# Second half of the Fourier gate computed between the second and the third branch, the Fourier branch stored ungated during the first block

## The chip, the cores and the metric

The kernel runs on one core of a Trainium2 chip. The core has five engines that work side by side, each through its own list of instructions in order: TensorE (PE, matmuls), VectorE (DVE), ScalarE (ACT), GpSimd (POOL) and SyncE (SP, which here only issues DMAs). The metric is the device time of one execution in microseconds (us).

## The reference

Two layers of a diffusion trunk over 512 sample tokens and 128 prompt tokens (640 columns), model width 1024, all in float32. In each layer the normalised hidden state `h` is projected by one wide matrix; three branches (retention, latent attention, Fourier mixing) are gated, projected and merged:

```
rq, rk, rv, rz, q_lat, kv_lat, k_r, mz, fu, fz, gl = jnp.split(h @ w_in, split_at, axis=-1)
o_r = retention(rq, rk, rv);  o_m = mla(q_lat, kv_lat, k_r);  o_f = fourier_mix(fu)
branches = jnp.stack([o_r * silu(rz), o_m * silu(mz), o_f * silu(fz)], axis=2)      # 3 x 512 wide
proj     = jnp.einsum('btnw,nwd->btnd', branches, w_branch)                         # 3 x 1024 wide
merged   = jnp.sum(proj * sigmoid(gl.reshape(B, T, 3, 1024)), axis=2)
x        = x + gate * (merged @ w_out)
```

## The kernel before

Everything lies transposed: features on the 128 partitions, tokens along the free axis. Each float32 operand is split into a rounded high part and a low rest (`split`: ACT casts the high part, `low` subtracts it on DVE or POOL, line 74), and each product is three matmuls (high x high, low x high, high x low).

A layer runs attention, retention, Fourier mixing, then the merge of the three branches, then the output projection. This case is about the passage from the Fourier mixing into the merge.

**The products of the merge.** `seven` makes 256 output features for all 640 tokens by seven block products in place of eight (a 2x2 block scheme: the weights and the tokens are added up beforehand). A block product of the hidden state is 12 matmuls of 128x320, so a gate (`gl`, or a quarter of `fz`) is 84 matmuls; a block product of a branch is 6, so a branch block is 42. `gl_weights` makes the weight sums of a gate from two loads (`raw`, `raw2`), `br_weights` those of a branch. The last two products of each `seven` are kept back in `tail` and run when `flush` is called, after the first product of the next one. `hq` holds the token sums of the hidden state. `branch_sums` makes the seven token blocks of a branch in place from its tile (lines 1008 to 1013) and splits each into two tiles: `bq0` to `bq9`, and four that don't fit and lie in `bql`. `bql` has the tag "of", the slot of the Fourier branch's own tile `oft`, so nothing can be written to `bql` before `oft` has been copied out to DRAM (`ofd`).

**The loops.** The Fourier branch has four groups of 128 features. `fourier` itself gates groups 0 and 1 (two `silu2`, line 954). Then one `seven` with its result in `zs` computes the gate of groups 2 and 3, `fourier_done` applies it (line 1234 and `fourier_gate`, line 954), and each group is stored to `ofd` (line 1236; groups 0 and 1 at line 1216). Then the merge: three branches in the order attention (n = 0, tile `omt`), retention (n = 1, tile `ort`) and Fourier (n = 2, loaded back from `ofd` into `ort` at line 1297), and for each of them four blocks of 256 output features: a gate (`seven`) and a branch product (`seven`, or `four` with 48 plain matmuls for n = 1). A gate's result is turned by ACT's tanh and multiplied in by DVE.

**What sets the order.** The source order is only a start: a list scheduler orders each engine's instructions when the program is built. Buffers rotate: `raw` 2, `raw2` 2, `wh` and `wl` (split weights) 4 each, `bank` (accumulators) 6, `th` 2. All loads of weights and all copies to and from `ofd` stand in SP's queue in order; the loads `mraw` of the modulation weights, which fill spare time on PE (line 187), stand in ACT's.

Of the kernel before, what the change touches and what calls it, by code (L numbers as in the profile page):

```python
# [8 lines left out]
F32 = mybir.dt.float32  # L9
# [21 lines left out]
def build(nc, tc, A, O):  # L31
# [806 lines left out]
    def fourier(l, fp, of, sums, wgp):  # L838
# [102 lines left out]
        ws = gl_weights(wgp, l, C_FZ + 256, lambda: z1.append(silu2(l, C_FZ + P, wz)))  # L941
# [50 lines left out]
    def branch_sums(gp, src, spare):  # L992
# [4 lines left out]
        t = t[:8] + x[:2] + t[8:] + x[2:]  # L997
# [195 lines left out]
    for l in range(DEPTH):  # L1193
# [21 lines left out]
        for w in range(2):  # L1215
            nc.sync.dma_start(ofd[:, w, :], oft[:, w, :])
# [3 lines left out]
        with ExitStack() as s:  # L1220
# [8 lines left out]
            zs = [fl.tile([P, TT], F32, name="tg", tag="th", bufs=2) for _ in range(2)]  # L1229

            def fourier_done(j):
                z, m, o = zs[j], mg[j], off[j + 2]
                ACT.activation(m, z, AF.Tanh, scale=0.5)
                DVE.scalar_tensor_tensor(m, m, 1.0, z, op0=ALU.add, op1=ALU.mult)
                fourier_gate(off, j + 2, m)
                nc.sync.dma_start(ofd[:, j + 2, :], o)

            seven(w0, hq, *zs, lambda ps: ACT.copy(zs[0][:, b], ps), fourier_done, lambda i: None)
# [6 lines left out]
            def gates(y2, n, bq, parts, np_):  # L1245
                def last(ps):
                    ACT.activation(y2[0][:, b], ps, AF.Tanh, scale=0.5)

                def fin(j):
                    y = y2[j][:, a] if j == 0 else y2[j]  # L1250
                    ACT.activation(y, y, AF.Tanh, scale=0.5)

                def tick(i):
                    if i in (3, 6):
                        next(steps, None)
                    if i % 2 and len(bq) < np_:
                        with tc.issue_after(gated.ins):
                            bq.append(next(parts))

                return last, fin, tick  # L1260
# [17 lines left out]
            for n, (idx, src, tmp) in enumerate(((1, omt, None), (0, ort, om), (2, ort, om))):  # L1278
                if n:
                    flush()  # L1280
                parts = branch_split(gp, src) if n == 1 else branch_sums(gp, src, bql)
                np_ = 4 if n == 1 else 7
                bq = []
                for i in range(4):
                    if n and i % 2 == 0:
                        y2 = tmp[2:4]
                    else:
                        y2 = [fl.tile([P, TT], F32, name="tg", tag="th", bufs=2) for _ in range(2)]
                    seven(gl_weights(wgp, l, C_GL + D * idx + 256 * i), hq, *y2, *gates(y2, n, bq, parts, np_))
# [176 lines left out]
```

## Time and profile before

| | us |
|---|---|
| median of 3 runs | 1479.51 (1477.54 to 1480.52) |
| the profiled execution's own time | 1482.52 |
| its span, first to last instruction | 1480.7 |

The profile is of one execution, 1.8 us outside its span and 3.0 us above the median. PE is busy for 96% of the span, DVE for 69%, ACT for 51%. The merge of layer 0 stands at about 431 to 710 us of the span, that of layer 1 at about 1153 to 1416 us. A row of the timeline begins with its start and its length, and a bracket at its end gives the idle time of the engine before it and what ended it.

### The profile page before, as it was taken

Reading aid. Unit: us, or ns where it says so; the run is one execution under the profiler, and the core shown is the slowest. Engines: PE = TensorE matmul, PEld = TensorE weight load, DVE = VectorE, ACT = ScalarE, POOL = GpSimd, SP = SyncE. Lnnn points to the kernel's source line nnn. Section 1 sums busy time; section 2 is a strip of 40 time slices with the busy share of each in tenths; the row PEclk is TensorE's granted clock in tenths of the full one; section 3 lists DMA queues with packets and bytes.
Section 4 is the critical chain, followed back from the end, with each engine's and each line's share of the span. In section 5 each row is a group of like instructions: output and inputs, shape, how many; then the busy total and the mean of one; then the engine's idle time right before and its main releaser. Section 6 shows DMA issues by size and latency. Waiting matters only on the chain.

```text
span 1480.7 us, 25121 instructions
## 1 busy us (share of the span) xinstructions
PE 1416.7 (96%) x9761; PEld 1346.9 (91%) x9761; DVE 1024.6 (69%) x1894; ACT 758.5 (51%) x1635; POOL 241.8 (16%) x227
## 2 busy tenths in 40 slices
PE   5999999999999999999999999999999999999997
PEld 3989989988897898999999899899889889999997
DVE  5367776667886686698573777765759768779843
ACT  6357666544544453455344566664545445445542
POOL 1220100301102111122312100021110112112240
PEclk9999999999999999999999999999999999999999
DMA  9520002421326464133532100042222424333342
GB/s 330 164 76 1 15 15 78 121 76 41 93 90 189 143 192 122 51 86 93 171 104 83 34 15 15 15 137 75 74 72 65 154 82 116 95 82 86 90 125 86
DMA packets 173735, 138.91 MB, mean 94 GB/s; under 512 B 8240, under 2 KB 164528, under 8 KB 173616
## 3 DMA queue, kind: packets, MB, share of 16 engines
q1 hardware_dynamic: 155568, 120.16, 28.0%
q10 hardware_dynamic: 18048, 17.15, 3.7%
q8 instruction: 77, 1.26, 0.4%
q14 instruction: 42, 0.34, 0.1%
HBM read 125.98 MB, written 11.30 MB: 93 GB/s over the span
## 4 chain that ended last, share of the span: by engine, by line
PE 72%; DVE 13%; DMA 6%; ACT 4%; issue 4%; POOL 1%; SPq 0%; POOLq 0%; DVEq 0%; ACTq 0%
PE bank L1109 25%; PE sm L85 5%; PE sm L87 5%; PE sm L86 5%; PE bank L1080 4%; PE big L513 4%; PE fill L319 3%; PE big L269 3%; PE sm L319 3%; PE sm L534 3%; DVE wl L74 2%; PE sm L526 2%; DMA mraw<-in_w_mod 2%; PE fill L187 1%; DMA raw<-in_w_in 1%
## 5 line engine op out<-in xcount | busy, mean ns | idle before, releaser
L74 DVE TENSOR_TENSOR wl<-raw,wh 128x1024 fp32r<-128x1024 f32 (+5 forms) x146 | 156.2, 1072 | 92.1 <-ACT wh L78 45.1
L78 ACT CAST wh<-raw 128x1024 fp32r<-128x1024 f32 (+5 forms) x126 | 104.4, 832 | 79.0 <-DMA raw<-in_w_in 18.1
L85 PE MATMUL sm<-wh,hh 128*128 128x256 f32 (+2 forms) x456 | 134.7, 296 | 0.4 <-DVE vl L74 0.4
L87 PE MATMUL sm<-wh,hl 128*128 128x256 f32 (+2 forms) x456 | 133.9, 294 | 0.9 <-DVE hl L74 0.9
L1109 PE MATMUL bank<-hh,wh 128*128 128x320 f32 x416 | 130.7, 316 | 4.0 <-ACT tg L1125 2.9
L86 PE MATMUL sm<-wl,hh 128*128 128x256 f32 (+2 forms) x456 | 134.5, 295 | 0.0
L1109 PE MATMUL bank<-hl,wh 128*128 128x320 f32 x416 | 129.5, 312 | 0.0
L1109 PE MATMUL bank<-hh,wl 128*128 128x320 f32 x416 | 127.8, 313 | 0.0
L74 POOL TENSOR_TENSOR wl<-raw,wh 128x1024 fp32r<-128x1024 f32 (+1 forms) x32 | 67.6, 2112 | 296.9 <-ACT wh L78 221.2
L74 POOL TENSOR_TENSOR wl<-st,wh 128x512 fp32r<-128x512 f32 x26 | 39.2, 1508 | 324.2 <-ACT wh L78 302.1
L85 PEld LDWEIGHTS sm<-wh,hh 128*128 128x128 f32 x456 | 88.2, 194 | 1.5 <-DVE vl L74 0.8
L87 PEld LDWEIGHTS sm<-wh,hl 128*128 128x128 f32 x456 | 88.0, 193 | 1.4 <-DVE hl L74 1.4
L86 PEld LDWEIGHTS sm<-wl,hh 128*128 128x128 f32 x456 | 88.4, 194 | 0.1
L1109 PEld LDWEIGHTS bank<-hh,wh 128*128 128x128 f32 x416 | 79.1, 190 | 9.9 <-ACT tg L1125 3.6
L1109 PEld LDWEIGHTS bank<-hl,wh 128*128 128x128 f32 x416 | 79.2, 190 | 0.0
L1109 PEld LDWEIGHTS bank<-hh,wl 128*128 128x128 f32 x416 | 78.7, 191 | 0.4 <-DVE raw L1025 0.4
L74 DVE TENSOR_TENSOR ptl<-sm,pth 128x384 fp32r<-128x384 f32 x128 | 67.4, 549 | 14.4 <-ACT pth L78 13.3
L1109 PE MATMUL bank<-bq,wh 128*128 128x320 f32 x320 | 72.1, 311 | 0.0
L78 ACT CAST pth<-sm 128x384 fp32r<-128x384 f32 x128 | 57.5, 480 | 24.1 <-PE sm L526 23.3
L78 ACT CAST wh<-st 128x512 fp32r<-128x512 f32 x68 | 39.7, 618 | 53.0 <-PE bank L1109 53.0
L640 DVE TENSOR_REDUCE nm<-big 128x1 f32<-128x768 f32 x64 | 60.7, 948 | 2.7 <-PE big L513 2.4
L74 DVE TENSOR_TENSOR wl<-st,wh 128x512 fp32r<-128x512 f32 x42 | 41.2, 980 | 30.2 <-ACT wh L78 27.7
(579 smaller groups left out, 4546.3 us busy)
## 6 DMA issues: line engine op xcount, KB each, us to landing
raw<-in_w_in SPq DMA_DIRECT2D x96, 512.0 KB, 4.0
mraw<-in_w_mod ACTq DMA_DIRECT2D x32, 512.0 KB, 4.3
raw<-in_w_branch SPq DMA_DIRECT2D x24, 512.0 KB, 3.6
raw<-in_w_out SPq DMA_DIRECT2D x16, 512.0 KB, 4.5
mraw<-in_w_mod SPq DMA_DIRECT2D x4, 1024.0 KB, 11.7
mraw<-in_w_mod SPq DMA_DIRECT2D x8, 512.0 KB, 8.3
raw<-in_w_in SPq DMA_DIRECT2D x8, 384.0 KB, 5.9
om<-xd SPq DMA_DIRECT2D x16, 192.0 KB, 3.1
```

The source lines that it names most:

```text
L74: eng.tensor_tensor(lo, src, hi.bitcast(F32), op=ALU.subtract)
L78: ACT.copy(hi, src)
L85: PE.matmul(out, ah, bh, start=first, stop=False)
L86: PE.matmul(out, ah, bl, start=False, stop=False)
L87: return PE.matmul(out, al, bh, start=False, stop=last)
L269: PE.matmul(ps[:, 512 * h:512 * h + 320], ws[a][:, k, :], xs[b][k][:, 320 * h:320 * h + 320], start=(first and k == 0 and i == 0), stop=(l ...
L319: PE.matmul(ps, w[a][:, k, :], (hh, hl)[b][k][:, hs], start=(k == 0 and i == 0), stop=(k == NK - 1 and i == 2))
L513: PE.matmul(S[:, 512 * h:512 * h + 384], qT[hd][a][:, t * P:(t + 1) * P], (kth, ktl)[b][hd % 3][:, 384 * h:384 * h + 384], start=(i == 0), ...
L534: PE.matmul(po[:, :256], vt[hd // 4][kt][:, hd % 4, :], pts[hd, qb][b][kt // 3][:, kt % 3, :], start=(kt == 0 and b == 0), stop=(kt == 5 a ...
L640: DVE.tensor_reduce(nm, Sv, axis=AX.XY if len(Sv.shape) == 3 else AX.X, op=ALU.max, negate=True)
L1080: PE.matmul(A, ws[u][:, k, j * P:(j + 1) * P], xs[k][v][:, h, :], start=(k == 0 and i == 0), stop=(k == 3 and i == 2))
L1109: PE.matmul(ps, w[u], x[v], start=(first and k == 0 and j == 0), stop=(k == n - 1 and j == 2), skip_group_check=True)
```

## The change

The gate of groups 2 and 3 is no longer computed ahead of the merge. `fourier` now loads the weights of the first gate of the merge in the place of those of the Fourier gate. The Fourier tile is stored to `ofd` with groups 2 and 3 ungated (group 0 and 1 are gated as before), by four DMAs that are issued in the first gate of n = 0, in the order 2, 3, 0, 1. The `seven` of the Fourier gate stands between n = 1 and n = 2, writes its result to `om[2]` and `om[3]` (free by then) and gates groups 2 and 3 in `ort`, after they were loaded back. Two smaller edits go with it: block 3 of `branch_sums` and not block 4 lies in `bql`, and in n = 0 every step of a gate may issue a part of `branch_sums`, not every second one. In n = 2 the gates of blocks 1 and 3, not 0 and 2, use `om[2:4]`.

```
@@ fourier
-        ws = gl_weights(wgp, l, C_FZ + 256, lambda: z1.append(silu2(l, C_FZ + P, wz)))
+        ws = gl_weights(wgp, l, C_GL + D, lambda: z1.append(silu2(l, C_FZ + P, wz)))
@@ branch_sums
-        t = t[:8] + x[:2] + t[8:] + x[2:]
+        t = t[:6] + x[:2] + t[6:] + x[2:]
@@ build
-        for w in range(2):
-            nc.sync.dma_start(ofd[:, w, :], oft[:, w, :])
...
-            zs = [fl.tile([P, TT], F32, name="tg", tag="th", bufs=2) for _ in range(2)]
...
-                z, m, o = zs[j], mg[j], off[j + 2]
+                z, m, o = om[2 + j], om[j], ort[:, 2 + j, :]
                 ACT.activation(m, z, AF.Tanh, scale=0.5)
                 DVE.scalar_tensor_tensor(m, m, 1.0, z, op0=ALU.add, op1=ALU.mult)
-                fourier_gate(off, j + 2, m)
-                nc.sync.dma_start(ofd[:, j + 2, :], o)
-
-            seven(w0, hq, *zs, lambda ps: ACT.copy(zs[0][:, b], ps), fourier_done, lambda i: None)
+                DVE.scalar_tensor_tensor(o, o, 0.5, m, op0=ALU.mult, op1=ALU.mult)
+
...
-                    if i % 2 and len(bq) < np_:
+                    if not n and not bq and not i:
+                        for w in (2, 3, 0, 1):
+                            nc.sync.dma_start(ofd[:, w, :], oft[:, w, :])
+                    if (i % 2 or not n) and len(bq) < np_:
...
+                if n == 2:
+                    seven(gl_weights(wgp, l, C_FZ + 256), hq, om[2], om[3], lambda ps: ACT.copy(om[2][:, b], ps), fourier_done, lambda i: None)
...
-                    if n and i % 2 == 0:
+                    if n and i % 2 == n - 1:
...
-                    seven(gl_weights(wgp, l, C_GL + D * idx + 256 * i), hq, *y2, *gates(y2, n, bq, parts, np_))
+                    seven(w0 if not (n or i) else gl_weights(wgp, l, C_GL + D * idx + 256 * i), hq, *y2, *gates(y2, n, bq, parts, np_))
```

In layer 0, SP's queue around the copies to `ofd` reads so before, with `in_w_branch` the weights of a branch block and `in_w_in` those of a gate:

```order
L92 DMA raw_5405<-in_w_branch 128x4x256
L1216 DMA ofd0_5103<-of_2986 128x640 x2
L92 DMA raw_5471<-in_w_in 128x8x128
L92 DMA raw_5601<-in_w_branch 128x4x256
L1236 DMA ofd0_5103<-of_2986 128x640
L1030 DMA raw2_5708<-in_w_in 128x8x128
L1236 DMA ofd0_5103<-of_2986 128x640
```

and now:

```order
L92 DMA raw_5275<-in_w_branch 128x4x256
L841 DMA traw_4568<-in_k_dftf 128x256
L1030 DMA raw2_5578<-in_w_in 128x8x128
L92 DMA raw_5341<-in_w_in 128x8x128
L1253 DMA ofd0_5103<-of_2986 128x640 x4
L92 DMA raw_5471<-in_w_branch 128x4x256
```

The four copies now stand together, ahead of the second branch block's weights.

In layer 1, ACT's list reads so at the start of the merge before (`wh_13338` are weights of the first gate, `bq6` and `bq2` high parts of the attention branch, L1117 and L1125 copies of a gate's product out of its accumulator):

```order
L1117 COPY tg_13249<-bank_13251 128x320
L78 CAST wh_13338<-st_13343 128x512
L78 CAST wh_13338<-st_13342 128x512
L78 CAST bq6_13326<-om_165 128x640
L78 CAST bq2_13322<-om_165 128x640
L1125 COPY tg_13250<-bank_13251 128x320
```

and now, where the gate is that of the attention branch's first block:

```order
L1117 COPY tg_13256<-bank_13258 128x320
L78 CAST bq6_13252<-om_165 128x640
L78 CAST wh_13398<-raw_13394 128x256
L78 CAST wh_13398<-raw_13394 128x512
L78 CAST bql_13245<-om_165 128x640
L1246 ACTIVATE tg_13256<-tg_13256 128x320
L78 CAST bq2_13248<-om_165 128x640
L1125 COPY tg_13257<-bank_13258 128x320
```

`bql` has moved up from behind the whole first gate, and L1125 still stands behind `bq2`.

DVE's list in layer 0 before, around the end of n = 1 (`bq` are low parts of the Fourier branch in `or`, `wl_7206` weights of its first block):

```order
L74 TENSOR_TENSOR bq1_7052<-or_2985,bq0_7051 128x640
L74 TENSOR_TENSOR bq5_7056<-or_2985,bq4_7055 128x640
L1010 TENSOR_TENSOR or_2985<-or_2985 128x2x320
L74 TENSOR_TENSOR wl_7086<-raw_7061,wh_7085 128x1024
L74 TENSOR_TENSOR bq7_7058<-or_2985,bq6_7057 128x640
L1013 TENSOR_TENSOR or_2985<-or_2985 128x2x320
L74 TENSOR_TENSOR bq3_7054<-or_2985,bq2_7053 128x640
L74 TENSOR_TENSOR wl_7206<-st_7213,wh_7205 128x512
```

and now, one gate later (L1231 and L1232 apply the Fourier gate, `wl_7265` are weights of the gate of n = 2's second block):

```order
L1231 SCALAR_TENSOR_TENSOR om_165<-om_165 128x640
L1113 TENSOR_TENSOR om_165<-bank_6990,om_165 128x320
L1232 SCALAR_TENSOR_TENSOR or_2985<-or_2985,om_165 128x640
L1231 SCALAR_TENSOR_TENSOR om_165<-om_165 128x640
L1232 SCALAR_TENSOR_TENSOR or_2985<-or_2985,om_165 128x640
L74 TENSOR_TENSOR wl_7265<-raw_7260,wh_7264 128x1024
L1113 TENSOR_TENSOR tg_7028<-bank_7134,tg_7028 128x320
L74 TENSOR_TENSOR bq9_7026<-or_2985,bq8_7025 128x640
L1024 TENSOR_TENSOR raw_7260<-raw_7260,raw2_7262 128x512
L1025 TENSOR_TENSOR raw_7260<-raw_7260,st_7271 128x512
L74 TENSOR_TENSOR bq5_7022<-or_2985,bq4_7021 128x640
L1008 TENSOR_TENSOR or_2985<-or_2985 128x2x320
```

All of `branch_sums` but the first block now stands behind the gating of groups 2 and 3; before, its blocks 5 and 3 and the sums of lines 1008 and 1009 stood far ahead, in the first half of n = 1.

## Rows read from the trace of the kernel before

**Rows 1.** The page: busy time, share of the span and instructions of each engine.
```profile
PE 1416.7 (96%) x9761; PEld 1346.9 (91%) x9761; DVE 1024.6 (69%) x1894; ACT 758.5 (51%) x1635; POOL 241.8 (16%) x227
```
**Rows 2.** Whom PE waited for in layer 0's merge, 420 to 712 us: total, times, longest.
```profile
PE bank L1109 <- ACT bql L78: 2.1, 1, 2.1
PE bank L1109 <- DVE wl L74: 0.8, 1, 0.8
...
PE bank L1109 <- ACT tg L1125: 0.5, 1, 0.5
PE fill L187 <- DMA mraw<-in_w_mod: 0.4, 2, 0.2
PE bank L1109 <- ACT tg L1117: 0.4, 1, 0.4
```
**Rows 3.** The same for layer 1, 1100 to 1420 us.
```profile
PE bank L1109 <- ACT tg L1125: 2.4, 1, 2.4
PE bank L1109 <- ACT bql L78: 2.0, 1, 2.0
...
PE fill L187 <- DMA mraw<-in_w_mod: 0.6, 1, 0.6
```
**Rows 4.** Stretches of the span: busy PE, PEld, DVE, ACT, POOL; granted clock; DMA share, GB/s.
```profile
460.00:470.00 10.00, 7.66 (x57) 5.72 (x56) 3.84 (x9) 4.75 (x9) 0.17 (x1) 0.85 0.90 280
...
1160.00:1170.00 10.00, 7.62 (x48) 6.57 (x50) 8.77 (x14) 3.60 (x7) 0.00 (x0) 0.84 0.01 2
...
1180.00:1200.00 20.00, 17.41 (x112) 15.63 (x111) 10.92 (x19) 7.84 (x14) 3.21 (x2) 0.91 0.50 155
```
**Rows 5.** Timeline of ACT, layer 0: the first split into `bql`.
```profile
466.04 0.72 ACT L78 CAST bql<-om 128x640 fp32r<-128x640 f32 x1 [3.78 <-DMA ofd<-of]
```
**Rows 6.** Chain that ended last: start, length, what.
```profile
467.51 1.08 PE fill L187 x8
...
1181.33 7.76 DMA ofd<-of
...
1213.81 49.37 PE bank L1109 x336
```
**Rows 7.** The copies to `ofd`, both layers: from issue to landing.
```profile
DMA to landing us min/median/max: 2.2/4.1/7.8
```
**Rows 8.** Timelines of PE, DVE and POOL at layer 0's first gates.
```profile
431.54 0.31 PE L1109 MATMUL bank<-hh,wh 128*128 128x320 f32 x1
...
435.01 0.68 DVE L1025 TENSOR_TENSOR raw<-raw,st 128x512 f32<-128x512 f32 x1
...
436.34 3.40 DVE L74 TENSOR_TENSOR bq<-om,bq 128x640 fp32r<-128x640 f32 x3
...
443.07 0.81 DVE L1010 TENSOR_TENSOR om<-om 128x640 f32<-128x640 f32 x1
...
445.61 0.82 DVE L74 TENSOR_TENSOR bq<-om,bq 128x640 fp32r<-128x640 f32 x1
446.35 1.22 DVE L74 TENSOR_TENSOR wl<-raw,wh 128x1024 fp32r<-128x1024 f32 x1
...
448.08 0.48 DVE L1113 TENSOR_TENSOR tg<-bank,tg 128x320 f32<-128x320 f32 x1
...
436.34 1.98 POOL L74 TENSOR_TENSOR wl<-st,wh 128x512 fp32r<-128x512 f32 x1 [11.99 <-ACT wh L78]
```
**Rows 9.** Timeline of ACT, layer 1: a gate's copy out of its accumulator.
```profile
1165.24 0.42 ACT L1125 COPY tg<-bank 128x320 f32<-128x320 f32 x1
```
**Rows 10.** Columns of rows 4, layer 0, just after the passage from n = 1 to n = 2.
```profile
630.00:640.00 10.00, 10.00 (x70) 10.00 (x69) 9.61 (x17) 5.14 (x11) 3.10 (x2) 1.00 0.42 116
640.00:650.00 10.00, 10.00 (x70) 10.00 (x69) 9.71 (x15) 5.08 (x10) 3.08 (x2) 1.00 0.36 98
```
**Rows 11.** Timeline of DVE, layer 0: an early sum of the Fourier branch.
```profile
554.30 0.81 DVE L1009 TENSOR_TENSOR or<-or 128x640 f32<-128x640 f32 x1
```
**Rows 12.** The page's DMA issues by line: count, KB each, median us to landing.
```profile
raw<-in_w_in SPq DMA_DIRECT2D x96, 512.0 KB, 4.0
```

## The prediction

> **What bounds the kernel now.** I read the page first. PE is busy for 96% of the span and DVE for 69% [rows 1], so a change is worth what it adds to or takes from the idle time of PE, and what it does to PE's clock. The lists of whom PE waited for come next, for the merge of each layer [rows 2, 3]. The reader is to see how little there is: in layer 0 five waits stand at the start of the merge, 0.5, 0.8, 0.4 and 2.1 us and one of the two 0.2 us of the modulation load, 4.0 us together; in layer 1 three, 2.4, 2.0 and 0.6, 5.0 us together. All lie in the Fourier gate and the first block, none at the passage from n = 1 to n = 2. The stretches then show the clock [rows 4]. In the three stretches that hold a wait of 2 us or more its mean is 0.85, 0.84 and 0.91: behind each such wait PE runs for some us at the lower level, 1.2 GHz. That costs (1 - 0.85) x 10 = 1.5 us in layer 0, and 0.16 x 10 + 0.09 x 20 = 3.4 us in layer 1. So the whole place holds 5.5 us in layer 0 and 8.4 us in layer 1, 13.9 us of 1480.7, and no gain there can be larger.
>
> **What makes the wait on bql.** ACT's split into `bql` starts after 3.78 us of idleness, ended by the copy of `of` to DRAM [rows 5]. The chain shows that copy in layer 1, 7.76 us from issue to landing [rows 6]. It can't be issued before the Fourier gate has been multiplied in. This is the wait that the change is about.
>
> **Part 1: the copy is made early.** Groups 2 and 3 are complete when `fourier` ends, and group 1 is gated before the three attention splits of 436.34 us [rows 8]. The four copies therefore stand in SP's queue with nothing left to wait for at about 436.5 us. With the median of 4.1 us [rows 7] the last lands at 440.6. The first `bql` split now needs, besides, the sum of line 1009, which I put at 441.5, one sum ahead of that of line 1010 in part 2: the copy is no longer what it waits for. Only a landing like the slowest, 7.8, would hold ACT until 444.3, and with it the split `bq2` behind it in ACT's list, which PE wants in part 2: there the two splits and the accumulator copy of part 2 would then end at 444.3 + 0.72 + 0.72 + 0.42 = 446.2 in place of 444.2; that bound costs PE 2.0 us a layer, and I take 0 because only loads that were issued ten us earlier share the queues. Behind the copies SP holds the weights of the second branch block, which must wait anyway for the `raw` buffer that the first block's weights have until DVE has split them. So the waits of 2.1 and 2.0 us on `bql` go, and the lower clock behind them with them: 2.1 + 1.5 in layer 0, 2.0 + 1.8 in layer 1.
>
> **Part 2: one gate less of cover.** A gate is 84 matmuls, and 336 of them take 49.37 us [rows 6], 0.147 each: 12.3 us. In these 12.3 us DVE and ACT made the sums of the attention branch. Now the first branch product follows the first 48 matmuls of a single gate, and what was hidden must be looked for. In layer 0 the gate starts at 431.5 [rows 8]. Its 48 matmuls take 7.1, eight modulation matmuls 1.1 [rows 6], 13 branch matmuls 1.9, 12 of the gate 1.8, three more 0.4: at 443.8 PE wants the block that needs the sum of line 1010. DVE ended that sum at 443.07 + 0.81 = 443.9 before. Ahead of it its list loses about as much as it gains: a 512-wide rest for one of 1024 and two half-wide weight sums (-1.1), one 512-wide rest and two smaller sums (-1.7) against a weight sum, two rests of the branch weights and one split (+2.6), so -0.2. Three splits took 3.40 us beside a POOL instruction of 1.98 where one alone takes 0.82, and about 0.75 in a row [rows 8]. That surplus, 3.40 - 2.25 = 1.2 us, goes or stays as POOL's instruction, now some 4 us earlier, falls on other DVE work; I take half, 0.6. The sum ends at 443.1, the split of its high part (0.72 [rows 5]) and the accumulator copy behind it on ACT (0.42 [rows 9]) at 444.2, so PE waits 0.4 (bounds 0 and 1.0). With 0.4 for a modulation load (between the 0.2 of [rows 2] and the 0.6 of [rows 3]) 0.8 us remain of 5.5: a gain of 4.7.
>
> In layer 1 the 2.4 us wait on line 1125 is the point. ACT's copy there stands behind the split `bq2` before and now, and that split waits for line 1010. PE reaches the matmul that needs the copy at the same time as before (21 gate matmuls then, 3.1 us; eight modulation matmuls and 13 others now, 3.0). DVE's list ahead of line 1010 is shorter by 0.3, and POOL's share is again 0.6, so 2.4 becomes 1.5 (bounds 1.1 and 2.4). Whether the clock falls after 1.5 us no row shows: it did after waits of 2.0 and more [rows 3, 4], it didn't after 0.8 [rows 2]; 1.5 is nearer to the former, and I charge the 1.6 us of that stretch. With the 0.6 of the modulation load 3.7 us remain of 8.4: a gain of 4.7. Both layers together: 9.4 us.
>
> The Trainium skill bears on the 0.6: SBUF — State Buffer, section "Who interferes with whom", says that a DVE instruction with two SBUF inputs and a POOL instruction that reads SBUF exclude each other for the whole of an instruction, while a DVE instruction with one SBUF input is not touched. The 3.40 us beside POOL's 1.98 agree in kind, though less than the whole 1.98 was lost. By that rule the 1.2 us would go wholly where POOL's instruction now lies beside the gating of line 298, which reads one operand from PSUM, and the sum would gain another 0.4 in layer 0 and 0.6 in layer 1.
>
> **Part 3: the Fourier gate in its new place.** The 84 matmuls come back between n = 1 and n = 2, so the PE work is equal. What is new is a chain. Before, the sums of lines 1008 and 1009 ran at 553 to 555 us [rows 11], 68 us before use. Now all of `branch_sums` but its first block stands behind the gating of groups 2 and 3. From the end of the gate's last product DVE and ACT do in a row: an add 0.48, tanh 0.72 as the split of the same width, lines 1231 and 1232 0.82 each, a weight rest 1.22, an add 0.48, the split `bq9` 0.82, two weight sums 0.68 each, `bq5` 0.82 [rows 5, 8]: 7.5 us. PE has 42 matmuls to run meanwhile, 6.2 us; it waits 1.3. Then line 1008 (0.81) and the next split (0.72) give 1.5 against five matmuls, 0.7: another 0.8. That makes 2.1 a layer. DVE has no slack to catch up, being busy 9.61 and 9.71 of 10 us there [rows 10]. The nearest rows are the two gates in a row at the start of the merge before, where the waits other than that on `bql` were 1.7 in layer 0 and 2.4 in layer 1 [rows 2, 3]. I take 2.4 a layer, 4.8 together. Bounds: 0, since the matmuls of the second block's gate could fill in; and 3.4 + 1.7 = 5.1 a layer, if weight splits wait for buffers too (a first one for 0.6, a second for 0.7) and the waits join to one after which the clock falls. The lines 1231 and 1232 are the former 1234 and 954 and add no work.
>
> **The sum.** -9.4 + 4.8 = -4.6 us: from the profiled execution's 1482.5 to 1477.9, and from the median of 1479.5 to 1474.9. I say 1475.
>
> **The rivals.**
> *The second place takes back what the first gives.* For it speaks DVE at 97% [rows 10] and the 2.1 us chain; against it that PE had no wait at all there before. With 4.0 a layer, and a first place that gains 8 only, the time is 1479.5, no change. The rule named above speaks for it too: POOL works 31% of that stretch, and the moved splits have two SBUF inputs each. By that rule the moved DVE work, 8 x 0.82 = 6.6 us a layer, would lose up to 31%, 2.0 us, and the time would be near 1479.
> *Slower.* The weights of n = 2's second gate are loaded into the `raw` buffer of its first gate, which is free only when DVE has split that gate, and now the splits `bq9` and `bq5` stand behind the rest of these weights. A load lands in 4.0 us as a median [rows 12], but the copy in [rows 6] took 7.76. It decides from a landing about 2 us later than the median: then PE waits 2.4 + 3.8 with the clock falling (1.7), 7.9 a layer, 15.8 - 9.4 = +6.4 us, 1486. Against it: the queues carry 98 to 116 GB/s there [rows 10], with 155 and 280 where landings were long [rows 4].
> *The second place is hidden wholly*, since the scheduler puts other matmuls of gates there: -9.4, 1470.
> *The first place keeps a wait on the copy* (the change doesn't do what it says): the landing of 7.8 us in both layers costs 2.0 each, and with the clock falling in layer 0 too 1.5, so -9.4 + 5.5 + 4.8 = 0.9 us and again no change; its chance is in that of the first rival.
>
> **How the numbers follow.** Chances: the forecast 0.45 (1472 to 1478.5), taking back 0.25 (1476.5 to 1482.5), slower 0.15 (1482.5 to 1488), hidden wholly 0.15 (1466 to 1472). The range of 8 in 10 is 1468 to 1482.5: it leaves out most of the slower case and a tip of the hidden one. No change means within 0.2%, 3.0 us, about what a measurement of this kernel can tell: 1476.5 to 1482.5. Faster: 0.15 + 0.35 of the forecast's 0.45 = 0.50. Same: 0.10 + 0.25 = 0.35. Slower: 0.15.
>
> **What would show it.** Right: no wait of PE on `bql` in n = 0, ACT's `bql` split not ended by `ofd`; the stretches of layer 0 at 460 to 470 at a clock of 1.0; one wait on line 1125 of 1 to 2 us left in layer 1; and at the passage to n = 2 new waits of PE on `bq` splits, 2 to 3 us a layer in pieces below 2 us. Wrong: a wait on `ofd` that stays, a piece above 2 us with the clock below 1.0 after the passage, a wait on `raw` there, or longer waits at the output projection, where a late DVE would show.

## The result and the profile after

The changed kernel takes 1495.82 us, the median of four runs (1494.37 to 1499.2), beside 1480.01 us of the kernel before on the same chip: a ratio of 1.0109, 95% interval 1.0091 to 1.0128. It is slower by 1.1%, where 1475 was forecast. The profiled execution took 1495.6 us with a span of 1493.8.

The page's busy times hardly move against [rows 1]; PE did the same 9761 matmuls:

```profile
PE 1421.0 (95%) x9761; PEld 1347.0 (90%) x9761; DVE 1028.0 (69%) x1894; ACT 760.0 (51%) x1635; POOL 236.0 (16%) x227
```

So the time must be looked for stage by stage. I cut each merge at four matmuls of PE's timeline: the first of a gate, the first branch matmul of n = 1 (line 1080), the last one of n = 1, and the last of the merge. For layer 0 of the changed kernel they are (start, length, what):

```profile
433.14 0.31 PE L1109 MATMUL bank<-hh,wh 128*128 128x320 f32 x1
...
535.18 0.42 PE L1080 MATMUL bank<-bq,wh 128*128 128x320 f32 x1
...
609.71 0.31 PE L1080 MATMUL bank<-bq,wl 128*128 128x320 f32 x1
...
710.33 0.31 PE L1109 MATMUL bank<-bql,wl 128*128 128x320 f32 x1
```

The same four from each timeline give this table. The Fourier gate, 12.3 us of matmuls by [rows 6], lies in the first stretch before and in the third after, so the column "net" has it taken out.

| us | before, layer 0 | after | net | before, layer 1 | after | net |
|---|---|---|---|---|---|---|
| up to this merge | 431.5 | 433.1 | +1.6 | 450.9 | 451.4 | +0.5 |
| first stretch: to the first product of n = 1 | 118.6 | 102.0 | -4.3 | 110.0 | 92.8 | -4.9 |
| second: n = 1's products | 73.6 | 74.8 | +1.2 | 67.0 | 67.0 | 0 |
| third: from there to the end | 78.4 | 100.6 | +9.9 | 78.2 | 101.2 | +10.7 |

With PE's work behind layer 1's merge, to its last matmul (64.2 before, 62.5 after), this sums to 13.0 us, and the spans differ by 13.1. What lies up to layer 0's merge took 431.4 to 436.0 us in the profiles of this study; PE's first 400 matmuls, while the first weights arrive, were over at 74.9 to 78.1 us and hold up to 3.2 us of that. So below I compare the stretches first, and the medians only beside them. Two things are to be seen: the first place gained what was forecast, 9.2 us for 9.4, and the third stretch lost 20.6 where the forecast had 4.8.

Whom PE waited for in the changed kernel, layer 0, 430 to 600 us (total, times, longest), to be held against [rows 2]:

```profile
PE fill L187 <- DMA mraw<-in_w_mod: 0.3, 1, 0.3
```

In layer 1, 1160 to 1310 us, against [rows 3]:

```profile
PE bank L1109 <- ACT tg L1125: 1.7, 1, 1.7
PE bank L1109 <- ACT wh L1033: 0.2, 1, 0.2
```

And in layer 0 from 605 to 722 us, where before only 0.6 and, at the output projection, 0.7 us stood:

```profile
PE bank L1109 <- DVE bq L74: 2.8, 1, 2.8
PE bank L1109 <- ACT om L1131: 2.2, 2, 2.0
PE bank L1109 <- ACT tg L1131: 1.4, 1, 1.4
PE sm L86 <- DVE hl L82: 1.0, 1, 1.0
PE bank L1109 <- ACT bq L78: 0.9, 2, 0.5
PE sm L85 <- ACT hh L81: 0.6, 1, 0.6
...
```

No wait on `bql` is left. New are two places: the passage to n = 2 (1.4, 2.8 and 0.9 us, 5.1 together; 4.4 in layer 1), and the end of the merge, where PE waits 2.0 us (2.5 in layer 1) for an accumulator copy. Behind the passage the clock falls, which it did not in [rows 10]: stretches as in [rows 4], layer 0 and layer 1:

```profile
640.00:650.00 10.00, 6.70 (x34) 6.17 (x33) 10.00 (x15) 3.91 (x7) 2.94 (x2) 0.83 0.20 52
...
1350.00:1360.00 10.00, 6.83 (x33) 6.01 (x32) 10.00 (x14) 5.17 (x9) 2.94 (x2) 0.83 0.28 74
```

PE ran 34 matmuls in ten us there, where it can run 70. A third stretch without any wait would take 78.4 - 0.6 + 12.3 = 90.1 us; that is the yardstick for the experiments. The stretches of the changed kernel lie 10.5 and 11.1 us above it, and PE's timeline accounts for that: waits at the passage 5.1 and 4.4, waits behind it 2.3 and 2.8, the lower clock 1.7 and 2.7 (1.0 of layer 1's at the end of the merge, where the clock is 0.90 from 1413 to 1423 us), and 1.4 and 1.2 in matmuls around the waits that followed each other more slowly than the usual 0.15 us.

Here is the passage on DVE and POOL (layer 0), and PE's two waits behind it:

```profile
632.46 0.69 DVE L1023 TENSOR_TENSOR st<-st,raw 128x512 f32<-128x512 f32 x1 [1.94 <-DMA raw<-in_w_in]
633.07 0.68 DVE L74 TENSOR_TENSOR wl<-raw,wh 128x512 fp32r<-128x512 f32 x1
633.67 0.82 DVE L1231 SCALAR_TENSOR_TENSOR om<-om 128x640 f32<-128x640 f32 x1
634.40 0.48 DVE L1113 TENSOR_TENSOR om<-bank,om 128x320 f32<-128x320 f32 x1
634.81 1.52 DVE L1232 SCALAR_TENSOR_TENSOR or<-or,om 128x640 f32<-128x640 f32 x1
...
640.71 1.77 DVE L1025 TENSOR_TENSOR raw<-raw,st 128x512 f32<-128x512 f32 x1
642.40 1.88 DVE L74 TENSOR_TENSOR bq<-or,bq 128x640 fp32r<-128x640 f32 x1
644.20 0.81 DVE L1008 TENSOR_TENSOR or<-or 128x640 f32<-128x640 f32 x1
...
633.67 1.96 POOL L74 TENSOR_TENSOR w<-raw,w 128x512 fp32r<-128x512 f32 x1 [4.71 <-ACT w L78]
640.42 1.50 POOL L74 TENSOR_TENSOR wl<-st,wh 128x512 fp32r<-128x512 f32 x1 [4.79 <-ACT wh L78]
642.16 1.44 POOL L74 TENSOR_TENSOR w<-raw,w 128x512 fp32r<-128x512 f32 x1 [0.23 <-ACT w L78]
...
644.33 0.41 PE L1109 MATMUL bank<-bq,wh 128*128 128x320 f32 x1 [2.80 <-DVE bq L74]
645.82 0.42 PE L1109 MATMUL bank<-bq,wh 128*128 128x320 f32 x1 [0.50 <-ACT bq L78]
```

Three candidates can be read off. DVE stands idle for 1.94 us until a weight load lands, with the first gating multiply (line 1231) behind it in its list. Three DVE instructions take 1.52, 1.77 and 1.88 us where their kind takes 0.82, 0.68 and 0.82: each ends about as long after a POOL instruction's end (635.63, 641.92, 643.60) as it takes alone, 0.70, 0.56 and 0.68 us later. And the chain itself is long, with line 1008's sum at its end. The texts written before each run call the chain theory A, GpSimd beside DVE (or DVE's fullness) theory B, the late load theory C, and the order at the end of the merge theory D.

### The profile page after: what moved, and what is told of

It reads as the page before. It is cut to its first block, busy times and chain, and to the rows that moved or that the text cites. A ratio compares the mean times of both kernels' runs of the same rounds, so it can differ in the third digit from the quotient of the medians.

```text
span 1493.8 us, 25101 instructions
## 1 busy us (share of the span) xinstructions
PE 1421.0 (95%) x9761; PEld 1347.0 (90%) x9761; DVE 1028.0 (69%) x1894; ACT 760.0 (51%) x1635; POOL 236.0 (16%) x227
## 4 chain that ended last, share of the span: by engine, by line
PE 69%; DVE 16%; issue 5%; DMA 5%; ACT 4%; POOL 1%; SPq 0%; POOLq 0%; ACTq 0%; DVEq 0%
PE bank L1109 23%; PE sm L85 5%; PE sm L87 5%; PE sm L86 5%; PE bank L1080 4%; PE big L513 4%; PE big L269 3%; PE fill L319 3%; PE sm L319 3%; DVE wl L74 3%; PE sm L534 2%; PE sm L526 2%; PE fill L187 2%; DMA raw<-in_w_in 1%; DMA mraw<-in_w_mod 1%
## 5 line engine op out<-in xcount | busy, mean ns | idle before, releaser
L74 POOL TENSOR_TENSOR wl<-raw,wh 128x1024 fp32r<-128x1024 f32 (+1 forms) x32 | 63.2, 1976 | 332.1 <-ACT wh L78 219.5
L1109 PEld LDWEIGHTS bank<-hh,wh 128*128 128x128 f32 x416 | 78.8, 190 | 11.8 <-ACT tg L1131 4.0
L1109 PE MATMUL bank<-bq,wh 128*128 128x320 f32 x320 | 73.6, 317 | 11.2 <-DVE bq L74 5.6
L74 DVE TENSOR_TENSOR wl<-st,wh 128x512 fp32r<-128x512 f32 x42 | 49.3, 1173 | 38.3 <-ACT wh L78 35.8
L1109 PEld LDWEIGHTS bank<-bq,wh 128*128 128x128 f32 x320 | 53.3, 189 | 17.2 <-DVE bq L74 6.5
```

The costliest lines, as they stand in the source:

```text
L74: eng.tensor_tensor(lo, src, hi.bitcast(F32), op=ALU.subtract)
L1109: PE.matmul(ps, w[u], x[v], start=(first and k == 0 and j == 0), stop=(k == n - 1 and j == 2), skip_group_check=True)
```

## The experiments

Each started from the changed kernel, but for the early copy alone, which started from the kernel before. The edits are shown in outline. The ratio is to the kernel before, with its interval; "third stretch" is that of the table, layer 0 and layer 1; the waits are those of PE.

**Without the gating multiplies.** Lines 1231 and 1232 taken out:

```
 ACT.activation(m, z, AF.Tanh, scale=0.5)
-DVE.scalar_tensor_tensor(m, m, 1.0, z, op0=ALU.add, op1=ALU.mult)
-DVE.scalar_tensor_tensor(o, o, 0.5, m, op0=ALU.mult, op1=ALU.mult)
```

> The changed kernel with the four multiplies of the Fourier gate (lines 1231 and 1232, two groups each) left out in both layers: the gate's product, its copies and its tanh are still made, and the branch goes ungated into the third block. The stretch read is from the last matmul of the second block's branch product to the last of the merge; it takes 100.6 us in layer 0 and 101.2 us in layer 1 of the changed kernel, with PE waits of 5.1 and 4.4 us at the passage. Theory A, the passage is lost to the chain behind the gating (gate, tanh, two multiplies a group, sums, splits): without the multiplies the sums don't wait for the gate, the passage's waits fall below 1 us a layer, and the stretch gets 5 to 7 us shorter in each layer; time 1481 to 1486 us. Theory B, DVE as a whole is too full there and any 3.3 us less would help by just that: 3 us a layer, 1489 to 1490 us. Theory C, late weights set the passage: under 2 us a layer, 1492 to 1496 us.

Measured: 1482.46 us (ratio 1.0018, 1.0004 to 1.0032); third stretch 94.6 and 94.4 us, 6.0 and 6.8 less. At the passage no wait is left at all; the wait for the copy at the end stayed, 2.6 and 2.4 us. So the passage is lost to what stands behind the gate, as theory A has it, and the end is a second thing. The run takes 3.3 us of work off DVE too; one that keeps the multiplies and only frees the sums from them was not made.

**Without GpSimd's splits from the Fourier gate on.**

```
 def low(eng, hi, lo, src):
+    if nopool and eng is POOL:
+        return ACT.copy(lo, src)
```

> The changed kernel, in which from the Fourier gate on to the end of the merge GpSimd makes no low part of the weights: ACT writes a copy in its place (the subtraction is left out in these tiles), so no GpSimd instruction of this kind lies beside a DVE instruction. In the changed kernel four DVE instructions at the passage of layer 0 took 1.52, 1.77, 1.88 and 1.78 us in place of 0.82, 0.68, 0.82 and 0.68, each beside such a GpSimd instruction. Theory B, this overlap is a main part of the loss: the passage's PE waits of 5.1 and 4.4 us fall by 2 to 3 us a layer and the clock stays up, so 4 us a layer with the end of the merge, time 1486 to 1489 us. Theory A, the length of the chain in DVE's list: the surplus is only moved, waits fall by under 1 us a layer, 1493 to 1496 us. ACT gets 0.6 us more for each of the splits, which the wait at the end may show.

Measured: 1484.73 us (1.0049, 1.0029 to 1.0069); third stretch 95.3 and 95.7, 5.3 and 5.5 less. The passage's waits fell from 5.1 to 3.0 and from 4.4 to 3.3 us, in pieces of at most 1.6, and the clock stayed up:

```profile
640.00:650.00 10.00, 7.73 (x49) 7.09 (x49) 10.00 (x18) 7.60 (x14) 0.00 (x0) 1.00 0.22 56
```

The wait at the end of the merge shrank too, to 0.6 us (the list of ACT had come out in another order), so not all of the 5.3 is the passage's. Line 1008's sum, on whose split PE's last wait at the passage ends, ended 32.9 and 33.0 us after the last product of n = 1, in place of 35.0 and 34.8. That is theory B: about 2 us a layer of chain, and the clock with it.

**DVE in GpSimd's place** (`eng = DVE` in the line above, so that nothing is left out):

> The changed kernel, in which from the Fourier gate on DVE itself makes the low parts that GpSimd made (two of 0.68 us for each gate, one for each branch product; about 9.5 us a layer more for DVE, which is busy 80 to 100 percent there). Theory B, each GpSimd split holds DVE for about what it takes DVE to do the same split itself (0.7 to 1.1 us were lost to each of the four at the passage): the passage is no worse than in the changed kernel and gets 1 to 3 us a layer shorter, 1487 to 1494 us. Theory A, DVE's own work is what is too much: the passage gets 2 us a layer longer and the rest of the third block starts to wait too, 1499 to 1510 us.

Measured: 1491.92 us (1.0087, 1.0069 to 1.0105); third stretch 99.8 and 99.4. Line 1008's sum ended at 32.9 and 33.2 us, as early as with that work left out, and the same instructions took their usual times:

```profile
640.92 0.69 DVE L1029 TENSOR_TENSOR raw<-raw,st 128x512 f32<-128x512 f32 x1
641.52 0.82 DVE L78 TENSOR_TENSOR bq<-or,bq 128x640 fp32r<-128x640 f32 x1
642.26 0.69 DVE L78 TENSOR_TENSOR wl<-st,wh 128x512 fp32r<-128x512 f32 x1
642.86 0.82 DVE L1012 TENSOR_TENSOR or<-or 128x640 f32<-128x640 f32 x1
```

So at the passage GpSimd's work cost DVE no less than doing it would have. What the stretch gave was only 0.8 and 1.8 us, since the end of the merge got later: PE waited 2.1 and 1.2 us there (1.6 and 1.4 in layer 1), and the clock fell behind these waits. At the passage it stayed at 1.00. Both theories have a part.

**Leaving a load out, twice.** I took DVE's idle 1.94 us first for the load of the third block's first gate, which was wrong:

```
-r1 = wraw(rows(A["w_in"][l], 0, NK, c0, P), NK, P)
+r1 = keep[0] if again else wraw(rows(A["w_in"][l], 0, NK, c0, P), NK, P)
```

> The changed kernel, in which the first of the two weight loads of the third block's first gate is left out: that gate takes the tile that the Fourier gate's first load left (other numbers, the same instructions). In the changed kernel DVE stood idle for 1.94 us in layer 0 and 1.71 us in layer 1 until that load landed, with the first multiply of the gating behind it. Theory C, the late load sets the passage: DVE's wait goes, the gating starts about 2 us earlier, the PE waits of 5.1 and 4.4 us fall by 2 us a layer and the lower clock behind them goes, 3 to 4 us a layer, time 1487 to 1490 us. Theories A and B, the load only fills time that DVE would lose to the chain or to GpSimd: less than 1 us a layer, 1494 to 1496 us.

Measured: 1497.8 us (1.0121, 1.0103 to 1.0138), third stretch 99.6 and 101.3, and DVE still waited 1.16 us at the same instruction. Then with the load that it did wait for:

> The changed kernel, in which the first weight load of the third block's second gate is left out (that gate takes the tile that the block's first gate was loaded into). The load of the run without a load before was not the one that DVE waited for: by the order of the loads, the 1.94 and 1.71 us of idle DVE ahead of the first gating multiply end with the load of the second gate, which can't be issued before DVE has split the third weights of the first gate. Theory C, this late load holds the gating: the wait goes, the gating starts about 2 us earlier, and the passage gets 2 us shorter, 3 to 4 with the clock, so that the third stretch is 97 to 99 us in place of 100.6 and 101.2; time 1488 to 1492 us. Rival: DVE is full behind it anyway and the chain of the gating sets the passage: under 1 us a layer, 1493 to 1497 us.

Measured: 1499.18 us (1.0136, 1.0119 to 1.0153); third stretch 101.4 and 102.9. DVE's wait was gone, and little came of it: line 1008's sum ended at 34.2 and 34.2 us, and PE waited 0.8, 1.6 and 2.2 us, 4.6 in all. Theory C falls. The loads were in time for all that PE wants.

**The gating ahead of the late sum**, by a written order:

```
+        with tc.issue_after(behind.pop()) if behind else ExitStack():     # behind: the last gating multiply
+            DVE.tensor_tensor(s2, s1, a11, op=ALU.subtract)
```

> The changed kernel with all its loads and results, in which DVE's sum that waits for the second gate's load stands behind the four gating multiplies, by an order written into the program. If what costs is that the waiting sum stands ahead of the gating in DVE's list (its operand, the tanh, was there 2.2 us before the multiply started), this gives what leaving out the load gives: 97 to 99 us for the third stretch, 1488 to 1492 us. If the load's lateness itself costs, because the second gate's weights come late for PE, the wait moves to that gate and the stretch stays at 100 us or more: 1494 to 1498 us.

Measured: 1500.14 us (1.0143, 1.0124 to 1.0163), third stretch 101.8 and 103.3. The gating was done at 636.5 in place of 637.9, and PE's waits became one:

```profile
640.03 1.79 DVE L1027 TENSOR_TENSOR raw<-raw,raw 128x512 f32<-128x512 f32 x1
641.74 1.75 DVE L1028 TENSOR_TENSOR raw<-raw,st 128x512 f32<-128x512 f32 x1
643.41 0.68 DVE L74 TENSOR_TENSOR wl<-st,wh 128x512 fp32r<-128x512 f32 x1
644.01 0.81 DVE L1008 TENSOR_TENSOR or<-or 128x640 f32<-128x640 f32 x1
...
645.64 0.41 PE L1112 MATMUL bank<-bq,wh 128*128 128x320 f32 x1 [4.18 <-ACT bq L78]
```

The work that had filled the time ahead of the gating now stands between it and line 1008, and POOL lies beside it again. The sum ended 34.8 and 34.8 us after the last product of n = 1, as in the changed kernel. By this run it is the amount of DVE's work up to line 1008 that counts, with what POOL adds to it, and not what stands first.

**The end of the merge.** In the changed kernel ACT does there

```profile
704.94 0.41 ACT L1125 COPY om<-bank 128x320 f32<-128x320 f32 x1
707.20 1.04 ACT L78 CAST wh<-raw 128x1024 fp32r<-128x1024 f32 x1 [1.85 <-DMA raw<-in_w_out]
708.15 0.42 ACT L1131 COPY om<-bank 128x320 f32<-128x320 f32 x1
...
708.62 0.56 PE L1109 MATMUL bank<-bq,wh 128*128 128x320 f32 x2 [1.95 <-ACT om L1131]
```

A split of the third output weights waits for its load, and the accumulator copy behind it, whose bank PE had filled, waits along. In the kernel before the copy stood ahead of the split:

```profile
699.09 0.42 ACT L1131 COPY om<-bank 128x320 f32<-128x320 f32 x1
700.67 1.05 ACT L78 CAST wh<-raw 128x1024 fp32r<-128x1024 f32 x1 [1.15 <-DMA raw<-in_w_out]
```

The written order:

```
+        copies.append(ACT.copy(y2[:, b], A))
 ...
+                    with tc.issue_after(copies[-1].ins):
+                        split(*w, rv, leng=eng)        # output weights 0 to 3
```

> The changed kernel, in which ACT's splits of the output weights that the merge's own buffers hold come behind the last accumulator copy (line 1131) of the merge, by an order written into the program. In the changed kernel such a split stood ahead of that copy and waited 1.85 us for its load; PE waited 1.95 us in layer 0 and 2.47 us in layer 1 for the copy. Theory D, this order at the end of the merge is a cost of its own, 2 us of waits a layer with some clock: the two waits go, the stretch to the end of the merge gets 2 us shorter a layer, and the time is 1491 to 1493 us. Rival: the loads then come late for the output projection, and what is won at the end of the merge is lost there: 1494 to 1497 us.

Measured: 1490.65 us (1.0079, 1.0059 to 1.0099); third stretch 96.9 and 96.9, 3.7 and 4.3 less; the wait is 0.5 us:

```profile
705.01 0.43 ACT L1131 COPY om<-bank 128x320 f32<-128x320 f32 x1 [2.21 <-PE bank L1109]
705.33 2.00 ACT L78 CAST wh<-raw 128x1024 fp32r<-128x1024 f32 x2
```

So theory D holds for the changed kernel as it is; 2.4 us of the 8.0 went again behind layer 1's merge (64.9 for 62.5), as the rival had it. But not all of the 3.7 and 4.3 us lies at the end. The waits behind the passage fell by 1.6 and 2.2 us, and in layer 1 1.0 us of lower clock went with them. The rest is at the passage, where DVE's list is the same. In layer 0 PE waited 3.4 us there in place of 5.1: POOL's splits fell beside other instructions (line 1231 took 1.92 us, line 1232 0.81 and line 1025 0.68). In layer 1 the wait of 2.8 us stood as before (window 1340 to 1360 us), and the clock stayed up this time, worth 1.7 us:

```profile
PE bank L1109 <- DVE bq L74: 2.8, 1, 2.8
...
1345.00:1355.00 10.00, 6.32 (x40) 5.53 (x39) 10.00 (x14) 5.46 (x10) 2.95 (x2) 1.00 0.28 79
```

That the order at the end did this is not shown. What it is worth by itself is thus some 1.6 and 3.2 us.

**Pairs, and all three.**

> As the run with DVE in GpSimd's place, and with the output weights' splits on ACT behind the last accumulator copy of the merge, which alone took the third stretch from 100.6 and 101.2 us to 96.9 and 96.9. If the two losses (the passage, and the order at the end) are separate, their gains add: the stretch is 94 to 95 us in each layer, about what leaving GpSimd's work out gave by itself, and the time is 1483 to 1487 us. If DVE is the bound over the whole third block, the end is late anyway: 97 us or more, 1490 us or more.

Measured: 1488.55 us (1.0065, 1.0047 to 1.0084); third stretch 97.1 and 97.4. The gains do not add, but not because the end is late, as the expectation had it: PE waits only 0.5 us there for the last copy, or 0.8. At the passage it waits 3.1 and 3.6 us, about as with DVE in GpSimd's place alone, but 2.3 and 2.4 of it in one piece, and behind that the clock falls (0.83 from 635 to 645 us).

> Both orders written in: the gating ahead of the late sum, and the last accumulator copy ahead of the output weights' splits. The latter alone gave 3.7 and 4.3 us a layer. If the two are separate, the third stretch is 93 to 95.5 us, and the time 1482 to 1486 us, still above the kernel before. If one thing is behind both, 96 to 97 us and 1489 to 1491 us.

Measured: 1495.76 us (1.0116, 1.0096 to 1.0137); 99.5 and 99.7. The expectation was written before the run with the gating first was known, and fell with it: that order costs 2.6 and 2.8 us beside the other alone, and 1.2 and 2.1 by itself. With the gating first in both, PE waits 5.1 to 5.2 us at the passage with and without the pinned copy, so this pair gives the end's order its cleanest price: 2.3 and 3.6 us.

> Both orders, and GpSimd's low parts from the Fourier gate on left out (copies by ACT in their place, another result). If the three causes named so far (the late load ahead of the gating, GpSimd beside DVE, the order at the end) make up the whole loss, the third stretch comes near its work alone, which is 78.4 - 0.6 + 12.4 = 90.2 us: 90 to 92 us in both layers, and with what the first place gains the time is 1471 to 1475 us, under the kernel before. If a part of the passage is the length of the chain itself, 93 us or more, and 1477 us or more.

Measured: 1484.91 us (1.0036, 1.0022 to 1.0049); third stretch 94.9 and 94.3. Against the run with the same two orders that is 4.6 and 5.4 us less, GpSimd's price with the end mended; against the run that only leaves GpSimd's work out it is 0.4 and 1.4 less, all that the two orders then still give. Some 4.8 and 4.2 us over the 90.1 stay, most of it in PE's waits at the passage (1.2, 0.8, 0.8 and 0.5 us in layer 0, 2.9 together in layer 1). That speaks for the rival, the length of the chain itself.

**The gate one block earlier**, between the third and the fourth gate of n = 1:

```
+if n == 1 and i == 3:
+    seven(gl_weights(wgp, l, C_FZ + 256), hq, om[2], om[3], ..., fourier_done, ...)
-if n == 2:
-    seven(gl_weights(wgp, l, C_FZ + 256), hq, om[2], om[3], ..., fourier_done, ...)
```

> The changed kernel, with the Fourier gate's block and its gating moved one more step ahead: between the third and the fourth gate of the second block, behind the reload, so that 126 matmuls and more lie between the gating and the third block's sums. Buffers alternate as before the change. Theory A with B (the passage is lost because the gating, the sums and their splits stand in a row on DVE, stretched by GpSimd): here the sums and gating are off that chain, so the passage's PE waits go as in the kernel before, and the first place keeps its gain: the merge takes 102.0 + 73.6 + 12.4 + 78.4 = 266.4 us in layer 0 and 92.8 + 67.0 + 12.4 + 78.2 = 250.4 us in layer 1, 4.2 and 4.8 us less than before; time 1470 to 1473 us. If the wait at the end of the merge comes with the change itself and not with its passage, 4 to 6 us of that are lost again: 1475 to 1478 us. Rival: a Fourier gate anywhere without a second gate in front of its gating costs the passage's 7 us a layer wherever it stands; then the second block shows the waits, and the time is 1484 to 1490 us.

Measured: 1483.98 us (1.0024, 1.0003 to 1.0046); merges 271.5 and 254.2 us. The end's wait is gone (third stretch 78.8 and 79.1), but the passage is not free: PE waits 2.0 us there, the clock falls, and second and third stretch together are 5.2 and 5.1 us longer than before with the gate's 12.3 added. That is nearer to the rival than to theory A. DVE is idle first and full afterwards, in stretches as in [rows 4]:

```profile
600.00:610.00 10.00, 10.00 (x70) 10.00 (x70) 3.66 (x5) 3.94 (x7) 0.00 (x0) 1.00 0.36 97
...
630.00:640.00 10.00, 8.03 (x43) 7.54 (x42) 10.00 (x18) 4.22 (x8) 0.00 (x0) 0.83 0.10 23
```

The sums still come behind the gating, and one block more was not room enough for both.

**The early copy alone**, on the kernel before. The gate's halves are made in `mg[4]` to `mg[7]`, which n = 0 doesn't write before its third block, and kept in `om[2]` and `om[3]`, once the attention branch is split (so the gates of n = 1 and n = 2 take `om[2:4]` in the other blocks):

```
+for w in (2, 3, 0, 1):
+    nc.sync.dma_start(ofd[:, w, :], oft[:, w, :])
+seven(w0, hq, mg[4], mg[5], ...)        # first, as before the change
 ...
+if not n and i == 1:                    # DVE, two instructions
+    om[2 + j] = (mg[6 + j] + 1) * mg[4 + j]
 ...
+if n == 1 and i == 0:                   # behind the reload, two instructions
+    ort[2 + j] = 0.5 * ort[2 + j] * om[2 + j]
```

> The early copy alone: the kernel before, in which the Fourier branch is copied to DRAM ungated as soon as it is complete, and the Fourier gate stays at the start of the merge as cover; its value is kept in the buffers of the attention branch, once these are free, and is multiplied in after the reload in the second block. The first place's waits on the split into the spare tile and the lower clock behind them are what the copy cost: 2.1 + 1.5 us in layer 0 and 2.0 + 1.8 in layer 1 by my prediction. If the prediction's reading of the first place is right, the first stretch (118.6 and 110.0 us before) gets 3 to 4 us shorter in each layer, nothing is lost at the passage, and the time is 1471 to 1474 us. Rival: the wait only moves to the next late thing there (the sums on DVE): 1 us a layer or less, 1477 to 1480 us.

Measured: 1472.09 us (0.995, 0.9934 to 0.9966), faster than both kernels. Merges 265.8 and 247.8 us, 4.8 and 7.4 less than before (the first stretch 7.9 and 9.2 shorter, the second 3.1 and 1.8 longer; twelve gate matmuls, 1.8 us, now run in the second and not in the first). PE's waits in layer 0, 430 to 720 us, and the gating and the first sum of the Fourier branch on DVE (the sum's row gives its times in both layers):

```profile
PE sm L86 <- DVE hl L82: 0.7, 1, 0.7
PE bank L1109 <- ACT om L1131: 0.6, 1, 0.6
PE bank L1109 <- ACT mg L1125: 0.5, 1, 0.5
PE bank L1109 <- ACT wh L78: 0.2, 1, 0.2
```

```profile
535.45 0.83 DVE L1295 SCALAR_TENSOR_TENSOR or<-or,om 128x640 f32<-128x640 f32 x1 [0.17 <-DMA or<-ofd]
```

```profile
L1008 DVE TENSOR_TENSOR or<-or x2: 820/820/821, 551.4 to 1260.0; 128x640 f32<-128x640 f32 x2
```

The gating is done some 85 us ahead of the passage, and the sum of line 1008 stands at 551.4 again, as its neighbour did in [rows 11].

## Why the prediction was wrong

**Part 1, the copy, was right.** ACT's first split into `bql` no longer waits for a DMA; it starts at 443.4 us behind an accumulator copy, against 466.04 [rows 5]. The 4.1 us of [rows 7] that I took is the median of the eight copies and the eight loads back together; the copies alone had 4.8 before, and now 5.7, with 7.6 at the longest. The last one landed at 439.9 us in layer 0, where I had 440.6, and nobody waited. The early copy alone confirms it from the other side: it gave 12.2 us of the 13.9 that I put on the place, and kept the gate as cover.

**Part 2, one gate less of cover, was right in its sum, in part by luck.** Forecast 4.7 us of gain a layer, measured 4.3 and 4.9. In layer 0 0.3 us of waits stay (0.8 forecast), in layer 1 one of 1.7 on line 1125 (1.5 forecast). I had charged a fall of the clock behind it; it stayed at 1.00 there. By the waits and the clock alone the first stretch should then have gained 0.9 us more in layer 0 and 1.6 in layer 1 than it did; that loss, which I had not foreseen, stands where I had the fall of the clock. Besides, n = 1 of layer 0 took 1.2 us longer. A part of the 1.2 is that n = 1 now holds 522 matmuls for 518: four of the modulation (line 196) came over from the first stretch, so layer 0's 4.3 us are a little too good. Where the rest is I have not found.

**Part 3 is the step that failed: the 2.4 us a layer at the passage, with bounds of 0 and 5.1.** Measured were 9.9 and 10.7 us in the third stretch, of which the passage's waits and the clock behind them are 6.8 and 6.1. The mechanism, gating ahead of the sums, was the right one, and four terms were missing or too small.

The chain: from the end of the gate's last product (633.0 in layer 0) to that of line 1008's sum I had 7.5 + 0.8 = 8.3 us, and it took 12.0. Of the 3.7 us that it is longer, up to 2.9 are the surplus of the three instructions beside POOL, (1.52 + 1.77 + 1.88) - (0.82 + 0.68 + 0.82); the rest lies in the late start, since DVE's add began 1.4 us behind the product. Even without POOL's part the chain cost more than my 2.4: 3.0 and 3.3 us of waits.

GpSimd: I had its surplus as a rival at 2.0 us a layer and left it out of the sum. Without it line 1008's sum ended 0.9 to 2.2 us earlier in four runs, two of them with DVE doing that work itself, and leaving the work out was worth 4.6 to 5.5 us a layer with the clock and the rest of the stretch. The Trainium skill, SBUF — State Buffer, section "Who interferes with whom", calls the port pair that the two engines share an exclusive lock. The rows agree: a DVE instruction with two SBUF inputs ended 0.6 to 0.7 us behind POOL's own end, as if it had begun there.

The clock: I expected waits in pieces below 2 us. They joined to one of 2.8, and behind it PE ran for some us at the lower level, 1.7 us a layer by the 0.83 of that stretch. I had this in the bound of 5.1 and not in the value. Behind the same wait the clock did not fall in layer 1 of the run with the pinned copy, so this term does not come each time.

The end of the merge: no step of mine looked there. The moved instructions let the scheduler place one split ahead of one copy on ACT, 2.0 and 2.5 us of waiting, and 2.3 and 3.6 us by the pair of runs whose passages waited alike. My last line did name longer waits at the output projection as a sign of a late DVE, and they are there in layer 0 (1.0 and 0.6 us for 0.7), not in layer 1. Why the scheduler chose that order is not settled. The terms overlap and can't be added as they stand: with GpSimd's splits out, both orders together are worth at most 0.4 and 1.4. Taken away one after the other, GpSimd first (5.3 and 5.5), then both orders (0.4 and 1.4), 4.8 and 4.2 us are left of the 10.5 and 11.1 by which 100.6 and 101.2 exceed 90.1; 3.3 and 2.9 of them are waits at the passage, which I put down to the chain's length.

**The rivals.** "Slower" came closest in time, 1486, and had the wrong cause: the late load of the second gate that it described was there, 1.94 and 1.71 us of idle DVE, and leaving it out made nothing faster. "Taken back" had the right one, DVE's fullness and GpSimd, at 4.0 us a layer in place of some 10. That [rows 10] showed DVE at 97% was the warning: work of 3.3 us with a chain behind it was moved to where DVE had 0.3 to 0.4 us to spare in each ten, from a place where it had cover.

## What to carry to other kernels

A transfer that is late because it waits for a value can often be sent without it, and the value applied behind the transfer; it pays if the late multiplication lands where its engine has room and its reader is far off, as in the early copy alone, and costs more than it saves if readers follow at once. When work is moved to a stage, add up the whole list of its fullest engine from the moved instruction to the first instruction that the bound engine waits for, each at the length that it has beside its neighbours there, and read afterwards also the end of the stage, where a list scheduler may have set something else in front. An idle stretch with a named releaser is no cost until an experiment that removes it moves the end: here one of 1.9 us could go, and the wait stayed. And where two profiles differ in a stage, look first whether the clock fell in both: here that alone was 1.7 us behind one and the same wait.

## What the runs showed of the hardware

A wait of 1.7 us left the granted clock at 1.00 (PE busy 8.31 of 10 us in 1165 to 1175 us of the changed kernel), as did four waits within some eight us, 3.0 us together and none above 1.5, in the run without GpSimd's splits. One wait of 2.8 us was followed by 0.83 in the changed kernel, in both layers, while in layer 1 of the run with the pinned copy it was followed by 1.00. A fall came too behind two of 0.9 and 1.0 us, 1.5 us apart, in the run with the gate one block earlier (0.83, 8.03 busy). So neither the sum nor the longest wait alone tells whether PE falls from 2.4 to 1.2 GHz.

POOL pays as well: the split that began at 633.67 us, together with line 1231, took 1.96 us, where 1.30 is its usual time in these traces.
